# An expert layer whose third weight pass is skipped by a branch for experts of at most 64 tokens

## The chip, the cores and the metric

The kernel runs on one core of a Trainium2 chip. The metric is the device time of one execution in microseconds, from three runs. A core has five engines that run their own queues in order and signal one another through semaphores: TensorE (PE, with the weight loads shown apart as PEld), VectorE (DVE), ScalarE (ACT), GpSimd (POOL) and SyncE (SP, which here issues the loads from HBM). Matmul results land in PSUM; everything else lives in SBUF, 128 partitions wide.

## What is computed

Two layers over 256 tokens of 1024 numbers. Layer 0 is a hybrid attention and a SwiGLU; layer 1 is a gated MLP over chunks and a mixture of eight experts, of which each token takes two. The change touches the experts alone:

```python
logits = xf @ w_router                       # 256 x 8
top_val, top_idx = lax.top_k(logits, 2)
gate = softmax(top_val)
# for each expert e, over the tokens that picked it:
y_e = (silu(x_e @ w_gate[e]) * (x_e @ w_up[e])) @ w_down[e]   # 1024 -> 3584 -> 1024
# y[token] = sum of gate * y_e over the token's two experts
```

All matrices are float32. The weights of one expert are 3 x 1024 x 3584 numbers, 44.04 MB; eight experts make 352 MB, which have to come from HBM once.

The number of tokens of an expert depends on the data. Running the reference's router on the inputs that setup_inputs() draws by default gives 59, 51, 67, 65, 51, 62, 83 and 74 tokens for experts 0 to 7.

## The kernel before

Float32 products are made from two float32r parts. Each operand is split into a high part (the operand rounded by a ScalarE cast) and a low part (operand minus high part, a subtraction on VectorE or GpSimd). A product is then three passes of matmuls into the same PSUM accumulator: high x high, high x low of the weights, low of the tokens x high of the weights.

`weights` (L95 to L130) brings in one weight tile of 1 MiB, 128 partitions x 2048 columns: a load on SP's queue into the next buffer of a ring of raw tiles, a cast on ScalarE into `wh` (L123), and a subtraction into `wl` on the engine asked for (L127). `cuts` says in how many pieces the cast and the subtraction are made; in the expert layer MOE_CUTS = (1, 1), one of each. The raw tiles have a ring of 14 buffers there (4 + 7 + 1 + W_BUFS_MOE = 2), `wh` and `wl` a ring of three each (WS_BUFS). A cast has to wait until TensorE is through with the tile three before it.

An expert has 128 slots for tokens. `gather` (L828) makes the tokens of the slots by matmuls with a 0/1 matrix, splits them into `xh` and `xl`, and keeps the way back. `expert_up` (L852) works in seven slabs of 512 hidden columns: for w_gate and for w_up two weight tiles each, and for each 128 rows three matmuls with the tokens as the stationary and 512 weight columns as the moving operand, into `ps_a`; then silu on ScalarE (L865) and the product on VectorE (L866). `expert_turn` transposes the slab on TensorE (L872) and splits it into `hh` and `hl` (`split_into`, L133 and L134). `expert_down` (L878) adds the slab's part of the down product, two weight tiles and 24 matmuls, into two `ps_d` accumulators; it runs one slab behind the up products (`late_down`). So an expert takes 42 weight tiles of 12 matmuls, 504 in all. `combine` (L895) spreads the expert's rows back over the tokens; GpSimd adds them to the sum `yacc` (L911).

The matmuls of one slab and the next follow one another on TensorE; the framework's scheduler orders the instructions of each engine ahead of time by its own estimate of durations, in the program's order of priority. `run_experts` (L958) goes over the experts; the gate weights are made in slab 3 of expert 0 (GATE_SLAB), the next expert's tokens are gathered in slab 5 (GATHER_SLAB). At the end a loop with a run-time count (L999) does the experts with more than 128 tokens again; there are none here, and it is jumped over.

Of the kernel before, what the change touches and what calls it, by code (L numbers as in the profile page):

```python
# [9 lines left out]
F32 = mybir.dt.float32  # L10
# [19 lines left out]
EPS = 1e-5  # L30
NEG = -1.0e30
# [9 lines left out]
# how many of a group's four heads the scalar engine scales, for each block of queries  # L41
ASIDE = dict(a=(1, 1), w=(0, 1), s=(2, 1))
GATE_SLAB, GATHER_SLAB = 3, 5
# [7 lines left out]
def tile_hybrid_gmlp_moe(  # L51
# [23 lines left out]
    # weights: rings of 8 KB buffers (raw, and the two parts), spread over the pools that exist at the time  # L75
# [18 lines left out]
    def weights(src, a, b, lo_engine=V, loads=1, cuts=(2, 4), behind=None):  # L94
        """src as two float32r parts whose sum is src; loaded and split in as many pieces as asked for, each equal  # L95
        share of the pieces queued behind what one entry of behind has for their engine."""
# [106 lines left out]
    def mm_rows(accs, lhs_h, lhs_l, parts, first, last, done=None):  # L203
        """accs[b][half][t, 512] += x[:, k]^T w[k]; parts: (wh, wl, row chunks) of weight tiles, one block at a time."""
# [18 lines left out]
    def rows_2k(w, g, lo_engine=V):  # L223
        """rows g * 256 to g * 256 + 255 of a matrix of D columns"""
# [7 lines left out]
    def mm_cols(acc, lhs_h, lhs_l, w, js):  # L232
        """acc[col, t] = w[:, js]^T x, over the whole model dimension."""
# [13 lines left out]
    with ExitStack() as actx:  # L247
# [4 lines left out]
        # bias tables: -slope * distance, masked  # L252
# [7 lines left out]
        # compressed keys: token t against the last position of window c  # L260
# [14 lines left out]
        # sel[r, c] = 1 where r is c or c + 32: adds the two parts of a stacked product  # L275
# [41 lines left out]
        # softmax of one group of four heads over dense keys: probabilities times `scale4`, transposed  # L317
# [142 lines left out]
                # gelu(z) = z / (1 + exp(-2 sqrt(2 / pi) (z + 0.044715 z^3)))  # L460
# [83 lines left out]
        # projections and attention, in the order that keeps the tensor engine fed  # L544
# [22 lines left out]
        # output projection, residual, norm  # L567
# [15 lines left out]
    with ExitStack() as fctx:  # L583
# [29 lines left out]
        def ffn_up_blocks(s):  # L613
            """the same, one block of tokens after the other"""
# [53 lines left out]
    with ExitStack() as gctx:  # L668
# [14 lines left out]
        # with the norm's gain and shift taken into the weights, it works from what the norm is taken of  # L683
# [185 lines left out]
    def expert_turn(sg):  # L869
        pt = ps_t()  # L870
        for i in range(4):
            PE.transpose(pt[:, i * P:(i + 1) * P], sg[:, i * P:(i + 1) * P], ident)  # L872
# [170 lines left out]
```

## Time and profile before

| | |
|---|---|
| median of 3 runs | 1482.59 us (1481.17 to 1483.14) |
| span of the profiled execution, first to last instruction | 1480.9 us |
| busy share of the span: PE, DVE, ACT, POOL | 96%, 80%, 64%, 12% |
| moved from HBM | 423 MB, 287 GB/s over the span |

The span stands 1.7 us below the median; what lies around the first and the last instruction is not in it. The page cuts the span into 40 slices: attention up to about slice 5, the SwiGLU up to slice 9, the gated MLP up to slice 12, then the experts. Busy times of PE are of overlapping matmuls, so 96% is not yet a proof that TensorE is the limit; the share of the granted clock was 0.986 over the span, that is 2.4 GHz nearly throughout. POOL's last GpSimd additions of each expert (L911) stand at a fixed place of each expert's work and so mark the experts' period.

### The profile page before, as it was taken

How to read it: one execution, taken by the hardware profiler on the slowest of the kernel's cores; microseconds unless marked ns; L12 is line 12 of the kernel's file. 1: busy time of each engine (PE TensorE's matmuls, PEld its weight loads, DVE VectorE, ACT ScalarE, POOL GpSimd, SP SyncE). 2: the span in 40 equal slices, each digit the busy share in tenths (PEclk: the TensorE clock that was granted, in tenths of full speed). 3: DMA queues.
4: the chain of work that ended last, by engine and by line, in shares of the span. 5: the costliest groups of instructions: out<-in, count | busy, mean ns of one | idle time of the engine just before them, and what ended most of it. 6: DMA issues, size and time to landing. Idle time of an engine off the chain costs nothing. (4 is left out here: it accounts for less than half of the span.)

```text
span 1480.9 us, 18693 instructions
## 1 busy us (share of the span) xinstructions
PE 1426.8 (96%) x7207; PEld 1186.0 (80%) x7207; DVE 1182.6 (80%) x1265; ACT 953.0 (64%) x920; POOL 174.3 (12%) x139
## 2 busy tenths in 40 slices
PE   8899999999979999999999999999999999999995
PEld 7887899997768887888788788878878887887883
DVE  7888855558667988888888888888888878888886
ACT  5677544443436767776776777777677667767772
POOL 8521100002050101000200200020020002002000
PEclk9999999999989999999999999999999999999998
DMA  9523975556558898999999999999999999999940
GB/s 274 175 88 98 351 261 185 198 171 214 179 190 295 313 358 312 358 364 329 328 364 342 330 351 361 346 328 368 339 325 365 363 335 331 363 351 323 353 191 31
DMA packets 198847, 425.72 MB, mean 287 GB/s; under 512 B 8472, under 2 KB 44368, under 8 KB 198752
## 3 DMA queue, kind: packets, MB, share of 16 engines
q1 hardware_dynamic: 196448, 419.71, 80.2%
q0 software_dynamic: 1248, 4.24, 1.0%
q8 instruction: 58, 0.95, 0.3%
q10 hardware_dynamic: 1056, 0.53, 0.1%
q14 instruction: 37, 0.30, 0.1%
HBM read 423.40 MB, written 1.05 MB: 287 GB/s over the span
## 5 line engine op out<-in xcount | busy, mean ns | idle before, releaser
L127 DVE TENSOR_TENSOR wl<-w,wh 128x2048 fp32r<-128x2048 f32 (+1 forms) x544 | 907.4, 1696 | 189.3 <-ACT wh L123 185.8
L123 ACT CAST wh<-w 128x2048 fp32r<-128x2048 f32 (+1 forms) x462 | 766.5, 1668 | 255.9 <-PE ps_a L862 102.3
L860 PE MATMUL ps_a<-wh,xhl 128*128 128x512 f32 x896 | 356.4, 398 | 0.0
L862 PE MATMUL ps_a<-wh,xhl 128*128 128x512 f32 x896 | 354.4, 396 | 0.0
L861 PE MATMUL ps_a<-wl,xhl 128*128 128x512 f32 x896 | 354.2, 395 | 0.0
L862 PEld LDWEIGHTS ps_a<-wh,xhl 128*128 128x128 f32 x896 | 168.4, 188 | 39.5
L861 PEld LDWEIGHTS ps_a<-wl,xhl 128*128 128x128 f32 x896 | 168.5, 188 | 38.5
L860 PEld LDWEIGHTS ps_a<-wh,xhl 128*128 128x128 f32 x896 | 168.4, 188 | 38.6
L892 PE MATMUL ps_d<-wl,hh 128*128 128x512 f32 x448 | 178.8, 399 | 0.0
L893 PE MATMUL ps_d<-wh,hl 128*128 128x512 f32 x448 | 176.8, 395 | 0.0
L891 PE MATMUL ps_d<-wh,hh 128*128 128x512 f32 x448 | 167.7, 395 | 0.4 <-ACT hh L133 0.4
L911 POOL TENSOR_TENSOR yacc<-yacc,part 128x512 f32<-128x512 f32 x28 | 65.4, 2356 | 796.9 <-ACT part L910 796.9
L236 PE MATMUL ps_a<-xth,wh 128*128 128x256 f32 x448 | 128.6, 288 | 3.1 <-DVE hg L471 3.1
L238 PE MATMUL ps_a<-xth,wl 128*128 128x256 f32 x448 | 128.5, 287 | 0.8 <-DVE wl L127 0.8
L237 PE MATMUL ps_a<-xtl,wh 128*128 128x256 f32 x448 | 127.7, 285 | 0.0
L891 PEld LDWEIGHTS ps_d<-wh,hh 128*128 128x128 f32 x448 | 84.2, 188 | 20.9 <-ACT hh L133 0.9
L892 PEld LDWEIGHTS ps_d<-wl,hh 128*128 128x128 f32 x448 | 84.3, 188 | 20.1 <-DVE wl L127 1.4
L893 PEld LDWEIGHTS ps_d<-wh,hl 128*128 128x128 f32 x448 | 84.3, 188 | 18.5
L236 PEld LDWEIGHTS ps_a<-xth,wh 128*128 128x128 f32 x448 | 86.5, 193 | 4.9 <-issue 3.7
L238 PEld LDWEIGHTS ps_a<-xth,wl 128*128 128x128 f32 x448 | 86.5, 193 | 2.5 <-issue 1.2
L237 PEld LDWEIGHTS ps_a<-xtl,wh 128*128 128x128 f32 x448 | 86.5, 193 | 0.9 <-DVE xtl L134 0.2
L127 POOL TENSOR_TENSOR wl<-w,wh 128x512 fp32r<-128x512 f32 (+1 forms) x56 | 65.8, 1209 | 69.8 <-ACT wh L123 69.7
(304 smaller groups left out, 1377.9 us busy)
## 6 DMA issues: line engine op xcount, KB each, us to landing
w<-in_moe_w_gate_dram SPq DMA_DIRECT2D x112, 1024.0 KB, 6.3
w<-in_moe_w_up_dram SPq DMA_DIRECT2D x112, 1024.0 KB, 7.3
w<-in_moe_w_down_dram SPq DMA_DIRECT2D x112, 1024.0 KB, 6.8
w<-in_ffn_w_gate_dram SPq DMA_DIRECT2D x11, 1024.0 KB, 5.6
w<-in_ffn_w_up_dram SPq DMA_DIRECT2D x11, 1024.0 KB, 9.3
w<-in_ffn_w_down_dram SPq DMA_DIRECT2D x11, 1024.0 KB, 6.2
w<-in_gmlp_w_in_dram SPq DMA_DIRECT2D x8, 1024.0 KB, 5.1
w<-in_att_w_in_dram SPq DMA_DIRECT2D x7, 1024.0 KB, 6.0
```

Of the source, the lines that this page charges most:

```text
L123: S.copy(wh_f[:, sl], w_f[:, sl])
L127: ins = lo_engine.tensor_tensor(wl_f[:, sl], w_f[:, sl], wh_f[:, sl].bitcast(F32), op=OP.subtract)
L236: PE.matmul(acc, wh[:, k, js], lhs_h[:, k, :], start=k == 0, stop=False)
L237: PE.matmul(acc, wh[:, k, js], lhs_l[:, k, :], start=False, stop=False)
L238: PE.matmul(acc, wl[:, k, js], lhs_h[:, k, :], start=False, stop=k == KD - 1)
L860: PE.matmul(acc, xh[:, k, :], wh[:, i, :], start=k == 0, stop=False)
L861: PE.matmul(acc, xh[:, k, :], wl[:, i, :], start=False, stop=False)
L862: PE.matmul(acc, xl[:, k, :], wh[:, i, :], start=False, stop=k == KD - 1)
L891: PE.matmul(accs[half], hh[:, k, :], wh[:, i, hs], start=s == 0 and k == 0, stop=False)
L892: PE.matmul(accs[half], hh[:, k, :], wl[:, i, hs], start=False, stop=False)
L893: PE.matmul(accs[half], hl[:, k, :], wh[:, i, hs], start=False, stop=last and k == 3)
L911: G.tensor_tensor(yacc[:, b, hs], yacc[:, b, hs], part[:, b], op=OP.add)
```

## The change

Three things change in the expert layer.

First, a branch. For experts 1 to 7, `few` is 1 where the expert has at most 64 tokens. Slots 64 to 127 of such an expert are empty, so the low parts of its tokens are put there: `gather` and `expert_turn` add `xl` (or `hl`) of slots 0 to 63, times `few`, to slots 64 to 127 of `xh` (or `hh`). The first pass then makes high x high in rows 0 to 63 and low x high in rows 64 to 127, and `add_halves` adds the two halves (times `few`) by a ScalarE copy and a VectorE addition. The third pass stands under `tc.If(many > 0)`, where `many` is a register of TensorE alone, loaded once per expert. With the tokens above, the branch skips it for experts 1, 4 and 5. Expert 0 has no branch and no halves, and keeps three passes.

Second, slabs of 1024 hidden columns (three, and one of 512) in place of 512. Tiles stay 1 MiB and 42 per expert; the passes of a tile are now run one after the other, eight matmuls each (four per branch and half in the last slab's down part). A row of w_gate and w_up read from HBM is 4 KB instead of 2 KB, and one partition of a w_down tile is 8 KB in one piece instead of two of 4 KB. Tiles are asked for up to three ahead (`take_tile`). W_BUFS_MOE goes from 2 to 1, GATE_SLAB to 1 and GATHER_SLAB to 2.

Third, GpSimd makes the low parts of the last 384 of the 2048 columns of each tile of the expert layer (not of the first three tiles and the last one), VectorE those of the other 1664.

```diff
-W_BUFS, W_BUFS_LATE, W_BUFS_MOE, WS_BUFS = 4, 7, 2, 3
+W_BUFS, W_BUFS_LATE, W_BUFS_MOE, WS_BUFS = 4, 7, 1, 3
+MOE_ASIDE = 384
...
-            sl = slice(i * a * b // cuts[1], (i + 1) * a * b // cuts[1])
+            sl = slice(i * (a * b - aside) // cuts[1], (i + 1) * (a * b - aside) // cuts[1])
...
+        if aside:
+            sl = slice(a * b - aside, a * b)
+            G.tensor_tensor(wl_f[:, sl], w_f[:, sl], wh_f[:, sl].bitcast(F32), op=OP.subtract)
@@ in gather
+        if few is not None:
+            V.scalar_tensor_tensor(xh[:, :, HALF:], xl[:, :, 0:HALF], few, xh[:, :, HALF:], op0=OP.mult, op1=OP.add)
+            V.scalar_tensor_tensor(back[HALF:, :], pt[0:HALF, :T], few[0:HALF], back[HALF:, :], op0=OP.mult, op1=OP.add)
@@ the branch, the halves, then expert_up
+    def low_half(many):
+        return nullcontext() if many is None else tc.If(many > 0)
+
+    def add_halves(acc, tmp, few):
+        S.activation(tmp, acc[HALF:, :], AF.Copy, scale=few[HALF:])
+        V.tensor_tensor(acc[0:HALF, :], acc[0:HALF, :], tmp, op=OP.add)
...
+                for k, j, acc, hs in each:
+                    PE.matmul(acc, xh[:, k, :], wh[:, j, hs], start=k == 0, stop=False)
+                with low_half(many):
+                    for k, j, acc, hs in each:
+                        PE.matmul(acc, xl[:, k, :], wh[:, j, hs], start=False, stop=False)
+                for k, j, acc, hs in each:
+                    PE.matmul(acc, xh[:, k, :], wl[:, j, hs], start=False, stop=k == KD - 1)
...
+                for h, acc in enumerate(accs):
+                    hs = slice(h * 512, (h + 1) * 512)
+                    if few is not None:
+                        add_halves(acc, sg[0:HALF, hs], few)
+                    S.activation(sg[:, hs], acc, AF.Silu)
...
+                add_halves(acc, tmp, few)
+                V.scalar_tensor_tensor(sg[:, hs], sg[:, hs], first, acc, op0=OP.mult, op1=OP.mult)
@@ in expert_turn
+            if few is not None:
+                V.scalar_tensor_tensor(h4[:, :, HALF:], l4[:, :, 0:HALF], few, h4[:, :, HALF:], op0=OP.mult, op1=OP.add)
@@ in expert_down
+            for k, j, wh, wl, acc, hs in each:
+                PE.matmul(acc, hh[:, k, :], wh[:, j, hs], start=s == 0 and k == 0, stop=False)
+            with low_half(many):
+                for k, j, wh, wl, acc, hs in each:
+                    PE.matmul(acc, hl[:, k, :], wh[:, j, hs], start=False, stop=False)
+            for k, j, wh, wl, acc, hs in each:
+                PE.matmul(acc, hh[:, k, :], wl[:, j, hs], start=False, stop=last and k == 2 * n - 1)
...
+                    more = nc.values_load(many_i[0:1, col], engines=[mybir.EngineType.PE], min_val=0, max_val=1,
```

## Rows read from the trace of the kernel before

**Rows 1.** Each engine's busy time in two of six experts' periods.

```profile
585.73:713.22 127.49, 126.60 (x575) 102.40 (x575) 108.05 (x63) 91.67 (x66) 9.34 (x5) 1.00 0.97 346
...
1223.40:1350.63 127.23, 126.26 (x576) 102.50 (x575) 107.49 (x61) 91.69 (x66) 9.31 (x5) 1.00 0.97 347
```

**Rows 2.** TensorE in order of time, start and duration, one matmul and the 17th after.

```profile
815.84 0.40 PE L891 MATMUL ps_d<-wh,hh 128*128 128x512 f32 x1
...
819.81 0.39 PE L893 MATMUL ps_d<-wh,hl 128*128 128x512 f32 x1
```

**Rows 3.** Groups of instructions in one expert's period (713.22 to 841.24).

```profile
L127 DVE TENSOR_TENSOR wl<-w,wh 128x2048 fp32r<-128x2048 f32 x43 | 99.7, 2323 | 19.1 <-ACT wh L123 18.9
L123 ACT CAST wh<-w 128x2048 fp32r<-128x2048 f32 x42 | 80.2, 1910 | 21.9 <-PE ps_a L862 13.1 <-PE ps_d L893 8.8
L861 PE MATMUL ps_a<-wl,xhl 128*128 128x512 f32 x113 | 44.6, 395 | 0.0
L134 DVE TENSOR_TENSOR hl<-ps_t,hh 128x512 fp32r<-128x512 f32 x7 | 4.8, 683 | 0.0
L866 DVE TENSOR_TENSOR sg<-sg,ps_a 128x512 f32<-128x512 f32 x7 | 4.8, 681 | 0.9 <-PE ps_a L862 0.9
```

**Rows 4.** SP's waits from 560 to 1400 us, and DMA at work in 4 us.

```profile
SPq L108 <- DVE wl L127: 717.5, 277, 5.4
...
468.00:472.00 4.00, 4.00 (x19) 3.25 (x18) 3.96 (x2) 2.81 (x2) 0.00 (x0) 1.00 1.05 401
```

**Rows 5.** VectorE in order of time around a GpSimd addition of an expert.

```profile
584.55 2.29 DVE L127 TENSOR_TENSOR wl<-w,wh 128x2048 fp32r<-128x2048 f32 x1 [1.29 <-ACT wh L123]
586.76 0.68 DVE L134 TENSOR_TENSOR y<-ps_d,y 128x512 fp32r<-128x512 f32 x1
588.00 3.40 DVE L127 TENSOR_TENSOR wl<-w,wh 128x2048 fp32r<-128x2048 f32 x1 [0.56 <-ACT wh L123]
```

**Rows 6.** GpSimd in the same stretch, and its durations in ns: minimum, median, maximum.

```profile
585.73 3.52 POOL L911 TENSOR_TENSOR yacc<-yacc,part 128x512 f32<-128x512 f32 x2 [87.30 <-ACT part L910]
...
L911 POOL TENSOR_TENSOR yacc<-yacc,part x28: 1273/2420/3355, 585.7 to 1357.4; 128x512 f32<-128x512 f32 x28
...
L127 POOL TENSOR_TENSOR wl<-w,wh x56: 721/1288/1750, 19.3 to 438.7; 128x512 fp32r<-128x512 f32 x40, 128x256 fp32r<-128x256 f32 x16
```

**Rows 7.** GpSimd's eight 256-column subtractions, and VectorE twice on one line.

```profile
421.93 6.93 POOL L127 TENSOR_TENSOR wl<-w,wh 128x256 fp32r<-128x256 f32 x8
...
426.99 1.29 DVE L187 SCALAR_TENSOR_TENSOR x_nat<-x_nat,ln,ln_gb 128x512 f32<-128x512 f32 x1
...
432.36 0.75 DVE L187 SCALAR_TENSOR_TENSOR x_nat<-x_nat,ln,ln_gb 128x512 f32<-128x512 f32 x1 [0.30 <-POOL ln L184]
```

**Rows 8.** VectorE and ScalarE groups by shape over the whole span.

```profile
L127 DVE TENSOR_TENSOR wl<-w,wh 128x512 fp32r<-128x512 f32 x212 | 140.3, 712 | 63.6 <-ACT wh L123 60.8 <-DMA w<-in_ffn_w_up_dram 2.4
L370 DVE TENSOR_TENSOR o_t<-ps_d,o_tmp 64x256 f32<-64x256 f32 x16 | 6.6, 415 | 3.7 <-ACT o_tmp L367 3.5
L367 ACT COPY o_tmp<-ps_d 64x512 f32<-64x512 f32 x8 | 4.7, 582 | 1.7 <-PE ps_d L541 1.4 <-DVE o_t L370 0.2
```

**Rows 9.** TensorE's sequencer at the loop's end: register load and branches, durations in ns.

```profile
L997 PEldq TENSOR_LOAD <-n_over_i x1: 484/484/484, 1464.5 to 1464.5; - x1
...
L999 PEldq COMPARE_BRANCH  x3: 97/185/3303, 1465.1 to 1476.8; - x3
```

**Rows 10.** TensorE's last two matmuls, in order of time.

```profile
1464.46 0.50 PE L904 MATMUL ps_t<-y,back 128*128 128x512 f32 x1 [0.75 <-DVE yacc L907]
1464.80 0.40 PE L905 MATMUL ps_t<-y,back 128*128 128x512 f32 x1
```

More of the change, by code (lines that the diff above doesn't have):

```diff
@@ L826, in take_of, with gather @@
         return take
-    def gather(n, take):
+    def gather(n, take, few=None):
         xhl = moe.tile([P, 2, KD, P], F32R, name="xhl", tag=f"xhl{n % 2}", bufs=1)
@@ new lines, in tile_hybrid_gmlp_moe, with up_src, down_src @@
+    slabs = [(c0, min(1024, FE - c0)) for c0 in range(0, FE, 1024)]
+    def up_src(w, s, i):
+        c0, wd = slabs[s]
+        a = 2048 // wd
+        return w[i * a * P:(i + 1) * a * P, c0:c0 + wd].rearrange("(k p) c -> p k c", p=P), a, wd
+    def down_src(w, s, i):
+        r0 = slabs[s][0] + i * 256
+        return w[r0:r0 + 256, :].rearrange("(p i) c -> p i c", i=2), 2, D
+    def low_half(many):
[3 more added lines that the diff above has]
+        V.tensor_tensor(acc[0:HALF, :], acc[0:HALF, :], tmp, op=OP.add)
@@ new lines, in expert_down @@
+    def expert_down(take_tile, s, hh, hl, accs, many):
+        last = s == len(slabs) - 1
+        n = slabs[s][1] // 256
+        got = [(i, *take_tile()) for i in range(n)] if last else [None] * n
+        for tiles, hfs in [(got, (0,)), (got, (1,))] if last else [([i], (0, 1)) for i in range(n)]:
+            if not last:
+                tiles = [(tiles[0], *take_tile())]
+            each = [(2 * i + j, j, wh, wl, accs[h], halves[h]) for i, wh, wl in tiles for j in range(2) for h in hfs]
+            for k, j, wh, wl, acc, hs in each:
[5 more added lines that the diff above has]
+                PE.matmul(acc, hh[:, k, :], wl[:, j, hs], start=False, stop=last and k == 2 * n - 1)
@@ L939, in tile_hybrid_gmlp_moe @@
     n_over_i = late.tile([P, 1], I32)
+    few = late.tile([P, NE], F32)
+    first = late.tile([P, NE], F32)
+    many_i = late.tile([P, NE], I32)
     def gate_weights():
@@ L956, in gate_weights, with fetch, take_tile @@
         V.tensor_copy(n_over_i, n_over)
+        V.tensor_scalar(few, lp[:, 0:NE], HALF + 0.5, None, op0=OP.is_lt)
+        V.tensor_scalar(first, few, -1.0, 1.0, op0=OP.mult, op1=OP.add)
+        V.tensor_copy(many_i, first)
+        V.memset(first[0:HALF, :], 1.0)
     def run_experts(todo, start_acc):
-        ready = [up_weights(todo[0][0], 0, kh, G, cuts=(2, 8), behind=[after[kh]]) for kh in range(2)] if start_acc else []
+        order = []
+        behind = None
+        for n, (w_gate, w_up, w_down, _, _) in enumerate(todo):
+            for s in range(len(slabs)):
+                order += [up_src(w, s, i) for w in (w_gate, w_up) for i in range(slabs[s][1] // 256)]
+                if behind:
+                    order += behind
+                behind = [down_src(w_down, s, i) for i in range(slabs[s][1] // 256)]
+        order += behind
+        ready = []
+        at = [0]
+        def fetch(*how, **kw):
+            if at[0] < len(order):
+                src, a, b = order[at[0]]
+                at[0] += 1
+                if at[0] == len(order):
+                    kw["cuts"] = (2, 4)
+                elif not how:
+                    kw["aside"] = MOE_ASIDE
+                ready.append(weights(src, a, b, *how, **{"cuts": MOE_CUTS, **kw}))
+        def take_tile():
+            while len(ready) < WS_BUFS and at[0] < len(order):
+                fetch()
+            return ready.pop(0)
+        if start_acc:
+            for i in range(2):
+                fetch(G, cuts=(2, 8), behind=[after[i]])
         take = take_of(todo[0][3])
-        ready += [up_weights(todo[0][1], 0, kh, cuts=MOE_CUTS, behind=[marks]) for kh in range(2)] if start_acc else []
-        gathered = [gather(0, take)]
+        if start_acc:
+            fetch(behind=[marks])
+        gathered = [(*gather(0, take), None, None, None)]
         late_down = None
@@ L967, in run_experts @@
             closing = n == len(todo) - 1
-            xh, xl, back = gathered[n]
-            for s in range(n_slab):
-                sg = expert_up(w_gate, w_up, s, xh, xl, ready)
+            xh, xl, back, few_n, first_n, many = gathered[n]
+            for s in range(len(slabs)):
+                sg = expert_up(take_tile, s, xh, xl, few_n, first_n, many)
                 if late_down:
```

88 lines of the change are left out of this document (39 added, 49 removed).

## The prediction

> **What bounds the kernel now.** The order in which to read is: the busy times by stretch, then the groups of one stretch, then the order of time around one event. GpSimd's additions into yacc come once per expert, so stretches cut at them are the experts' periods: six of them take 127.2 to 128.0 us, each with TensorE busy for all but 1 us at the full granted clock (1.00, 2.4 GHz), VectorE 108 us and ScalarE 91.7 us [rows 1]. Busy matmuls overlap, so the pace is taken from starts: 17 matmuls in 819.81 - 815.84 = 3.97 us, 0.2335 us each [rows 2]. An expert's 504 make 117.7 us; 28 transposes, 32 matmuls of the gather and the way back fill the rest. TensorE sets the period. VectorE and ScalarE wait for it: a cast waits for a buffer that TensorE still reads, VectorE waits for casts (19.1 us per expert) [rows 3]. Loads are not late: SP stands waiting for a free raw buffer 717.5 of 840 us [rows 4]. So a shorter TensorE helps until the next engine is late, and that one has only 127.5 - 108 = 19.5 us of room.
>
> **The change, part by part.** *Third pass skipped.* Three of seven branching experts (1, 4, 5; at most 64 tokens) lose 504/3 = 168 matmuls, 168 x 0.2335 = 39.2 us each: TensorE would need 88 us there, 127.5 us in experts 2, 3, 6, 7 and in expert 0. All seven have the same work on the other engines, for the halves are added whether few is 1 or 0.
>
> *ScalarE.* Added: 14 copies of 64 x 512 from PSUM per expert at 0.58 us [rows 8] = 8.1 us; 91.7 + 8.1 = 99.8 us. Below 127 us, and not first.
>
> *VectorE alone.* A subtraction costs 2.29 us undisturbed for 2048 columns [rows 5] and 0.71 us on average for 512 [rows 8], 1.05 ns a column with the averages (2.32 and 0.71); 384 fewer columns save 0.40 us, leaving 1.89 us, 42 x 0.40 = 16.9 us per expert. Added: 14 additions of halves at 0.68 us (the nearest rows, an addition with PSUM of 512 columns [rows 3]) = 9.6 us; 7 additions of hl into hh, 256 columns, 0.42 us by the 64 x 256 row [rows 8] = 2.9 us; 1.1 us in the gather. 108.0 - 16.9 + 13.6 = 104.7 us.
>
> *GpSimd's 384 columns.* This is the dear part. A yacc addition of 512 columns began at 585.73 while a VectorE subtraction ran (584.55 for 2.29 us); the two additions together end at 589.25, though one alone takes 1.27 us at least [rows 5, 6]: 1 us of those 3.52 was spent waiting for the subtraction's end. The subtraction that began at 588.00, just after the second addition had started, took 3.40 us instead of 2.29: it waited 1.11 us for GpSimd [rows 5, 6]. The VectorE operation in between, which reads one operand from PSUM, took its usual 0.68 us beside GpSimd's first addition [rows 5]. So in this trace operations whose two operands are both in SBUF take turns with GpSimd, in full, and those with an operand in PSUM do not. With 256 columns of GpSimd in the way a VectorE operation took 1.29 us instead of 0.75, a wait of 0.54 us [rows 7]. Between 0.54 us for 256 and 1.11 us for 512 columns, 384 hold VectorE up for about 0.83 us (an estimate halfway). It saves 0.40 us and costs a turn of 0.83 us.
>
> Turns per expert: 42 x (1.89 + 0.83) = 114.2 us; four yacc additions at 1.11 = 4.4 us; the hh additions and one of the gather, both operands in SBUF, 3.6 us. Sum 122.2 us. VectorE's other 32 operations of 0.68 us (7 products, 7 + 4 splits, 14 halves; 21.9 us) can run in GpSimd's turns. If all do, the two engines need 122.2 us; if none does, 144.1 us. A turn of 0.83 us covers one such operation, and there are 42 turns for 32, but they come in clumps (two additions and two products at the end of each w_up, split and hh addition after it), and a clump's second and third are not covered. I take two thirds covered: 122.2 + 7.3 = 129.5 us, 2 us over today's period, in all seven experts.
>
> The Trainium skill (SBUF — State Buffer, "SBUF: two separate sides") says that of a GpSimd operation and a VectorE operation with two SBUF inputs, the one that starts first holds the shared pair of ports for its whole instruction. The rows agree that one blocks, but the wait was 1.11 us of an instruction of at least 1.27; by the page's wording a turn would be about 1.00 us, midway between the durations for 256 and 512 columns, 42 x 0.17 = 7 us more per expert, some 50 us more in all.
>
> *Experts with three passes.* TensorE's 127.5 us and the pair's 129.5 us are nearly equal and linked by three weight buffers, so each waits for the other at times: 2 us more each is my estimate from one missed cast of 1.91 us [rows 3]. Expert 0 has no halves: 42 turns and 4 us make 118 us, TensorE keeps it at 127.5.
>
> *Branches.* 42 per expert on TensorE's sequencer, never seen inside a matmul stream here. The branches at the loop took 0.10 and 0.19 us, one 3.30 us [rows 9]. The register load began at 1464.5, when the matmul of 1464.46 had just started [rows 9, 10]: the sequencer doesn't wait for matmuls to end. If it runs ahead, branches cost nothing; if each join makes it wait for the last matmul, 0.40 us (a matmul's 0.395 us [rows 3]), 16.8 us per expert. I take zero. The register load, 0.48 us seven times, is 3 us at most, at zero if ahead.
>
> *Loads.* At 122 us an expert's 44.04 MB ask for 361 GB/s; 401 was moved in a stretch of full work [rows 4]. Larger pieces don't hurt. One raw buffer of 14 fewer costs nothing: SP waits for buffers, not for data [rows 4]. SP's queue holds only these loads.
>
> *Ring of three.* Cast 1.91, VectorE 1.89, GpSimd 0.83, matmuls 1.87 us make 6.5 us over three buffers, 2.2 us per tile, below 122.2 / 42 = 2.9. The first pass needs only wh.
>
> *Sum.* Experts 1, 4, 5: +2.0 each, not -39. Experts 2, 3, 6, 7: +4.0 each. The last expert's halves in the tail: 0.58 + 0.68, about 1 us. 6 + 16 + 1 = 23 us on the profiled 1480.9, which stands 1.7 us below the median: 1504 and, on the median, 1506 us.
>
> **Rivals.**
> *A. The turns fit.* If all of VectorE's PSUM operations fall into GpSimd's turns, the pair needs 122.2 us: experts 1, 4, 5 gain 5.3 us each, the others stay. 16 us less, 1467 us. For it: 42 turns for 32 operations, and ScalarE ahead. Against: VectorE works in order.
> *B. GpSimd doesn't hold up VectorE.* Then experts 1, 4, 5 go at VectorE's 104.7 us or a few more, say 111: 3 x 16.5 = 50 us less, 1433 us. Against it stand the waits of 1.11 and 0.54 us [rows 5 to 7]. This is also the sum that leaves the turns out.
> *C. The branches stop the stream.* 0.40 us at 42 joins in experts 2, 3, 6, 7 makes TensorE 144.3 us there, 67 us in all; in 1, 4, 5 88 + 17 is still covered. With 6 us for those three 1556 us. It decides from 0.05 us per join, where TensorE's 129.6 us passes the pair's.
> *D. Each skip fetches code.* If the taken branch costs the 3.30 us of the longest branch [rows 9], experts 1, 4, 5 need 88 + 42 x 3.30 = 227 us on TensorE, 298 us more in all, about 1780 us. The Trainium skill (Runtime: NRT & Kernel Launch, "Instruction fetch mechanics") says that a taken branch whose target lies outside the instructions at hand stalls for a fetch; the row of 3.30 us is a jump over a whole expert's code, while these skip eight matmuls, so few should.
> That the branch skips nothing would need other token counts; it would change little, as the pair is the limit.
>
> **How the numbers follow.** Forecast 0.53 (of it 0.07 within 0.2%, the smallest difference that a measurement of this kernel can tell), A 0.20, B 0.10, C 0.12, D 0.05. Faster by over 0.2%: A and B, 0.30. Same 0.07. Slower 0.46 + 0.12 + 0.05 = 0.63. The forecast's own range is 1485 (a quarter of the 21.9 us uncovered, no further waits) to 1540 (six tenths uncovered). The range goes from 1455 (A with 3 us more hidden in four experts) to 1568 (C with the register loads and some misses), leaving out B and D.
>
> **What would show it.** VectorE's 1664-column subtractions well above 1.89 us where they wait, GpSimd's above 1.0; experts 1, 4 and 5 no more than 5 us shorter than now, with TensorE idle a quarter of them and waiting for wl; the other experts 127 to 135 us. Wrong would be: undisturbed 1.89 us beside a working GpSimd and short periods of about 111 us (B), or gaps at the branch in TensorE's order of time (C, D).

## The result, and the profile after

The changed kernel takes 1543.6 us (median of four runs, 1541.6 to 1546.1) beside 1482.9 for the kernel before on the same chip: 1.0412 times as long (95% interval 1.0397 to 1.0428), 61 us more. Forecast was 1506 us, 23 more. The direction was right and the time lies in the range given, 1455 to 1568, but outside the forecast's own, 1485 to 1540, and 38 us of the loss are not in the sum.

Where it went, by expert: the time from the first up matmul of an expert to that of the next (for expert 7 to the end of the span), in us.

| expert | 0 | 1 | 2 | 3 | 4 | 5 | 6 | 7 to end |
|---|---|---|---|---|---|---|---|---|
| tokens | 59 | 51 | 67 | 65 | 51 | 62 | 83 | 74 |
| before | 119.0 | 127.5 | 127.3 | 127.5 | 127.3 | 127.3 | 127.2 | 149.8 |
| after | 120.4 | 125.2 | 135.5 | 136.6 | 140.1 | 134.4 | 138.4 | 165.4 |

Expert 0, without branch and halves but with the new slabs and GpSimd's share, stayed. Experts 2, 3 and 6 lost 8 to 11 us where 4 were forecast. Of the three that skip a third of their matmuls, 1 gained 2.3 and 4 and 5 lost 12.8 and 7.1, where 2 each were forecast. Expert 7 with the end of the kernel lost 15.6, the largest single part, where 5 were forecast.

The page of the changed kernel, busy times and the granted clock in 40 slices:

```profile
PE 1390.3 (90%) x6703; PEld 1085.7 (70%) x6703; DVE 1277.5 (83%) x1427; ACT 1004.5 (65%) x1017; POOL 903.6 (59%) x472
...
PEclk9999999999989999999999999999999999999997
```

Each engine's busy time in experts 2 and 4 of the changed kernel, which answer to [rows 1], and in two stretches of 8 us inside expert 4 (columns as there: stretch, its length, PE, PEld, DVE, ACT, POOL, clock, DMA share, GB/s):

```profile
692.16:827.68 135.52, 129.30 (x567) 99.78 (x566) 124.20 (x86) 99.03 (x79) 101.80 (x47) 1.00 0.89 328
964.27:1104.38 140.11, 111.42 (x416) 71.93 (x415) 122.47 (x86) 98.96 (x79) 99.60 (x47) 0.95 0.87 319
...
1000.00:1008.00 8.00, 5.01 (x18) 3.71 (x18) 3.96 (x4) 3.51 (x6) 7.13 (x5) 0.75 0.65 209
1008.00:1016.00 8.00, 6.29 (x19) 3.59 (x17) 7.16 (x7) 5.86 (x6) 2.83 (x2) 0.83 0.53 179
```

VectorE is busy 124.2 and 122.5 us here. That this is near the forecast's 122.2 for the pair is chance: VectorE's busy time holds the 22 us of operations with PSUM that the forecast's sum leaves out, and not the turns of GpSimd that VectorE did not wait for. What that sum means is the time in which GpSimd runs or VectorE runs an operation without PSUM. Counted from the start and end of each instruction in the trace it is 122.3 us in expert 2 and 123.8 in expert 4, so the sum was met. VectorE's PSUM operations add 9.3 and 10.6 us outside that time, where the forecast has 7.3 (two thirds covered), and for another 3.9 and 5.7 us neither engine works: 135.5 and 140.1 in all. A period read as the largest engine sum plus a third of the unhidden work misses what the engines wait for one another. From 1000 to 1008, just where expert 3's rows are spread back, VectorE is idle half the time and GpSimd alone is busy.

Groups of expert 4 in the changed kernel, which answer to [rows 3]:

```profile
L131 DVE TENSOR_TENSOR wl<-w,wh 128x1664 fp32r<-128x1664 f32 x43 | 98.9, 2331 | 9.8 <-ACT wh L127 9.4 <-issue 0.4
L136 POOL TENSOR_TENSOR wl<-w,wh 128x384 fp32r<-128x384 f32 x43 | 94.0, 2202 | 37.8 <-ACT wh L127 30.2 <-PE ps_a L893 5.9 <-PE ps_d L937 1.6
L875 ACT ACTIVATE tmp<-ps_a,few 64x512 f32<-64x512 f32 x7 | 4.8, 686 | 6.1 <-PE ps_a L893 6.0
L876 DVE TENSOR_TENSOR ps_a<-ps_a,tmp 64x512 f32<-64x512 f32 x7 | 4.8, 682 | 0.0
L924 DVE SCALAR_TENSOR_TENSOR hh<-hl,few,hh 128x256 fp32r<-128x256 f32 x7 | 4.8, 690 | 0.1
```

and VectorE's subtractions over the experts, minimum, median and maximum in ns:

```profile
L131 DVE TENSOR_TENSOR wl<-w,wh x281: 1871/2679/2953, 570.3 to 1477.6; 128x1664 fp32r<-128x1664 f32 x141
```

VectorE's subtraction of 1664 columns takes 2.33 us against 1.89 undisturbed. Where it waits, it mostly waits 0.8 us (2.68 at the median for 1.87 at the least), the turn that was forecast, but it waits at about every second tile, so 0.44 us a tile. The other side of the turn is the dearer one: GpSimd's 384 columns, 0.99 us at the least (below), take 2.20 us on average. The halves cost what was forecast, but for the copies (0.68 for 0.58 us) and the hh additions (0.69 for 0.42, turns among them).

What the engines of the changed kernel waited for from 600 to 1480 us (engine, what, for whom; us in total, times, longest):

```profile
PEld ps_a L893 <- DVE wl L131: 70.2, 82, 2.7
ACT hh L140 <- PE ps_d L942: 66.7, 19, 5.7
ACT sg L875 <- PE ps_a L893: 61.8, 20, 4.2
DVE wl L131 <- ACT wh L127: 56.0, 62, 4.2
ACT tmp L875 <- PE ps_a L893: 43.8, 23, 2.4
...
ACT part L959 <- POOL yacc L960: 23.7, 7, 4.8
...
PEld ps_t L920 <- ACT part L959: 20.0, 7, 5.0
...
PEld ps_t L920 <- PEq L938: 10.2, 14, 0.8
```

and in the kernel before, in the same stretch:

```profile
PEld ps_t L872 <- ACT part L910: 8.2, 6, 1.4
...
PEld ps_d L892 <- DVE wl L127: 1.4, 9, 0.2
```

Two circles can be read from these lines. In the first, ScalarE waits at the head of its queue for TensorE to finish a slab (66.7, 61.8 and 43.8 us for hh, sg and tmp), the casts behind it come late, VectorE waits for casts, and TensorE for VectorE. In the second, once per expert, ScalarE's copies into the one buffer of `part` wait for GpSimd's yacc additions, and TensorE's transposes wait for ScalarE to empty `ps_t`. The second is not new: the kernel before has the same wait, 1.4 us at the most where it is now up to 5.0.

The second circle in order of time, expert 4 of the changed kernel, which answers to [rows 5, 6]:

```profile
996.88 2.72 POOL L136 TENSOR_TENSOR wl<-w,wh 128x384 fp32r<-128x384 f32 x1 [3.75 <-PE ps_a L893]
...
999.56 4.15 POOL L960 TENSOR_TENSOR yacc<-yacc,part 128x512 f32<-128x512 f32 x2
...
1003.67 0.99 POOL L136 TENSOR_TENSOR wl<-w,wh 128x384 fp32r<-128x384 f32 x1
1003.74 1.26 ACT L959 ACTIVATE part<-ps_t,gate 128x512 f32<-128x512 f32 x2 [3.58 <-POOL yacc L960]
...
1004.48 1.98 PE L920 MATMUL ps_t<-ident,sg 128*128 128x128 f32 x8 [2.84 <-ACT part L959]
...
1006.27 0.69 DVE L141 TENSOR_TENSOR hl<-ps_t,hh 128x512 fp32r<-128x512 f32 x1 [3.68 <-ACT hh L140]
```

GpSimd's additions stand behind a share of 2.72 us and take turns with VectorE themselves; ScalarE stops for 3.58 us, TensorE for 2.84, VectorE for 3.68. In the kernel before GpSimd had nothing else to do there.

### The profile page after: what moved, and what is told of

It reads as the page before. It is cut to its first block, busy times and chain, and to the rows that moved or that the text cites. A ratio compares the mean times of both kernels' runs of the same rounds, so it can differ in the third digit from the quotient of the medians.

```text
span 1542.6 us, 19479 instructions
## 1 busy us (share of the span) xinstructions
PE 1390.3 (90%) x6703; PEld 1085.7 (70%) x6703; DVE 1277.5 (83%) x1427; ACT 1004.5 (65%) x1017; POOL 903.6 (59%) x472
## 5 line engine op out<-in xcount | busy, mean ns | idle before, releaser
L131 DVE TENSOR_TENSOR wl<-w,wh 128x1664 fp32r<-128x1664 f32 (+1 forms) x541 | 899.1, 1700 | 150.4 <-ACT wh L127 144.2
L136 POOL TENSOR_TENSOR wl<-w,wh 128x384 fp32r<-128x384 f32 x333 | 743.0, 2248 | 272.5 <-ACT wh L127 245.7
L127 ACT CAST wh<-w 128x2048 fp32r<-128x2048 f32 (+1 forms) x461 | 751.6, 1671 | 134.9 <-PE ps_d L653 25.2
L893 PE MATMUL ps_a<-wl,xhl 128*128 128x512 f32 x896 | 272.2, 419 | 42.8 <-DVE wl L131 38.0
L888 PE MATMUL ps_a<-wh,xhl 128*128 128x512 f32 x896 | 258.1, 405 | 8.8 <-ACT wh L127 8.6
L888 PEld LDWEIGHTS ps_a<-wh,xhl 128*128 128x128 f32 x896 | 168.5, 192 | 57.3 <-ACT wh L127 23.5
L891 PE MATMUL ps_a<-wh,xhl 128*128 128x512 f32 x560 | 153.6, 395 | 0.0
L191 POOL TENSOR_TENSOR ln<-ln,neg_half 128x1 f32<-128x1 f32 x10 | 9.6, 961 | 243.0 <-DVE ln L190 243.0
L942 PE MATMUL ps_d<-wl,hh 128*128 128x512 f32 x448 | 132.9, 416 | 16.4 <-DVE wl L131 11.4
L937 PE MATMUL ps_d<-wh,hh 128*128 128x512 f32 x448 | 127.7, 405 | 14.3 <-ACT wh L127 9.5
L891 PEld LDWEIGHTS ps_a<-wh,xhl 128*128 128x128 f32 x560 | 105.4, 188 | 24.5
L140 ACT CAST hh<-ps_t 128x512 fp32r<-128x512 f32 (+1 forms) x58 | 31.9, 581 | 79.9 <-PE ps_d L942 74.0
```

Source lines behind the costliest of these rows:

```text
L127: S.copy(wh_f[:, sl], w_f[:, sl])
L136: G.tensor_tensor(wl_f[:, sl], w_f[:, sl], wh_f[:, sl].bitcast(F32), op=OP.subtract)
L140: marks[S] = S.copy(hi, src)
L888: PE.matmul(acc, xh[:, k, :], wh[:, j, hs], start=k == 0, stop=False)
L891: PE.matmul(acc, xl[:, k, :], wh[:, j, hs], start=False, stop=False)
L893: PE.matmul(acc, xh[:, k, :], wl[:, j, hs], start=False, stop=k == KD - 1)
```

## The experiments

Theory T is the forecast's: the turns of VectorE and GpSimd are the loss. Its rivals changed as results came in. All runs were timed beside the kernel before (1481.6 to 1482.2 us); the ratio's 95% interval stands in brackets.

**Without GpSimd's share.** The line of the first is all its edit; in the second GpSimd writes zeros, so the low parts of these columns are left out.

```diff
-MOE_ASIDE = 384
+MOE_ASIDE = 0
@@ zeros_aside, in weights
-            G.tensor_tensor(wl_f[:, sl], w_f[:, sl], wh_f[:, sl].bitcast(F32), op=OP.subtract)
+            G.memset(wl_f[:, sl].bitcast(F32), 0.0)
```

> The changed kernel with all 2048 columns of the low parts on VectorE (GpSimd's share 0). Theory T (VectorE and GpSimd take turns and their joint work sets the experts' period): VectorE gains 42 x 0.40 = 17 us of work per expert and loses about as much waiting (18.5 us in expert 4), so the time stays within 15 us of the changed kernel's 1543.6: 1530 to 1555 us. Rival R1 (GpSimd's turns are the whole loss, VectorE alone has room): 1470 to 1500 us. Rival R2 (branches or the chain of the halves are the loss): 1535 to 1555 us, TensorE's waits for wl as long as now.

1512.2 us, 1.0203 [1.0186, 1.0220]: between the range of T and that of R1. The share costs 31 us; half of the loss is there without it.

> The changed kernel, but GpSimd writes zeros into the last 384 columns of wl instead of the subtraction; so the low parts of these columns' weights are left out of the products. GpSimd still writes 384 columns per tile and VectorE still does 1664, but GpSimd reads nothing. Theory T: VectorE's 1664-column subtractions fall from 2.33 to about 1.89 us, experts 1, 4, 5 take 115 to 122 us, the others 128 to 131: 1470 to 1500 us. Rival R2 (branches or the halves' chain): nothing gained, over 1525 us. If a write alone blocks VectorE as well, 1520 us or more with VectorE's subtractions still above 2.1 us.

1485.4 us, 1.0026 [1.0016, 1.0036], in T's range. VectorE's subtractions are back at 1.90 us although GpSimd still writes 384 columns per tile (expert 4):

```profile
L131 DVE TENSOR_TENSOR wl<-w,wh 128x1664 fp32r<-128x1664 f32 x42 | 78.5, 1904 | 13.2 <-ACT wh L127 7.6 <-POOL wl L136 4.5 <-issue 1.1
...
L136 POOL MEMSET wl<- 128x384 f32 x42 | 17.6, 420 | 97.7 <-PE ps_a L893 59.5 <-PE ps_d L942 34.6 <-DVE wl L131 3.7
```

With 384 columns off VectorE and no turns at the tiles, the changed kernel is 58 us faster and still no faster than the kernel before.

**Without branch and halves.** No expert gets `few`, `first` or `many`; slabs and pass order stay.

```diff
-                    got = gather(n + 1, take_of(todo[n + 1][3]), few[:, col])
+                    got = gather(n + 1, take_of(todo[n + 1][3]))
...
-                    gathered.append((*got, few[:, col], first[:, col], more))
+                    gathered.append((*got, None, None, None))
```

> Slabs of 1024 and GpSimd's 384 columns, but no branch and no halves: all experts make three passes, as expert 0 does in the changed kernel. Theory T: turns of 42 x 2.72 + 5 = 119 us plus some 4 us of uncovered PSUM operations stay under TensorE's 127.5 us: 1480 to 1495 us. Rival R1 (the turns alone): 1520 us or more. Rival R2 (branch or halves): 1480 to 1490 us.

1524.4 us, 1.0289 [1.0272, 1.0306]. T missed; the time lies in R1's range, but the next run shows that the share is 18 us of it and not the whole.

> Slabs of 1024 alone: no branch, no halves, nothing on GpSimd. All theories: TensorE sets 127.5 us per expert, 1478 to 1488 us. Over 1495 us the slabs or the order of the passes would themselves cost something.

1506.4 us, 1.0165 [1.0149, 1.0182]. Every theory missed: slabs of 1024 and the new pass order, which the forecast's sum has no term for, lose 25 us by themselves. ScalarE in order of time in this kernel (bracket: idle time before, and for whom):

```profile
951.53 0.59 ACT L140 CAST hh<-ps_t 128x512 fp32r<-128x512 f32 x1 [5.08 <-PE ps_t L920]
952.02 7.32 ACT L127 CAST wh<-w 128x2048 fp32r<-128x2048 f32 x4
962.90 1.09 ACT L901 ACTIVATE sg<-ps_a 128x512 f32<-128x512 f32 x2 [3.56 <-PE ps_a L893]
```

and in the kernel before:

```profile
949.56 0.59 ACT L133 CAST hh<-ps_t 128x512 fp32r<-128x512 f32 x1 [1.33 <-PE ps_t L872]
950.05 1.91 ACT L123 CAST wh<-w 128x2048 fp32r<-128x2048 f32 x1
952.36 1.91 ACT L123 CAST wh<-w 128x2048 fp32r<-128x2048 f32 x1 [0.40 <-PE ps_a L862]
955.16 0.60 ACT L865 ACTIVATE sg<-ps_a 128x512 f32<-128x512 f32 x1 [0.89 <-PE ps_a L862]
```

Before, casts and evictions alternate and each waits about a microsecond. After, the scheduler has put evictions ahead of casts that could have run: ScalarE stands 5.08 us and then makes four casts on end. By the trace, TensorE's last matmuls on the buffers that the first two of these casts refill (its low x high passes) ended at 947.3 and 950.1, 4.7 and 1.9 us before ScalarE got to the first cast. Experts 1 and 2, whose instructions stand in another order, ran at 126.5 and 126.2 us; experts 3 to 6, ordered as here, at 131.2 to 132.3.

**Which part of the slabs.** From three_passes_vector_alone: slabs of 512 (and with them the old places of the gate weights and of the gather), the old pass order, both, or tiles asked for one at a time.

```diff
-    slabs = [(c0, min(1024, FE - c0)) for c0 in range(0, FE, 1024)]
+    slabs = [(c0, 512) for c0 in range(0, FE, 512)]
-GATE_SLAB, GATHER_SLAB = 1, 2
+GATE_SLAB, GATHER_SLAB = 3, 5
@@ old pass order, in expert_up; expert_down alike
                 for k, j, acc, hs in each:
                     PE.matmul(acc, xh[:, k, :], wh[:, j, hs], start=k == 0, stop=False)
+                    PE.matmul(acc, xh[:, k, :], wl[:, j, hs], start=False, stop=False)
+                    PE.matmul(acc, xl[:, k, :], wh[:, j, hs], start=False, stop=k == KD - 1)
@@ tiles one at a time, in take_tile
-            while len(ready) < WS_BUFS and at[0] < len(order):
+            while len(ready) < 1 and at[0] < len(order):
```

> The changed kernel with slabs of 512 columns in place of 1024, three passes for every expert without branch and halves, VectorE alone for the low parts; of the change only the order of the passes, the fetching up to three tiles ahead and the two row orders are left. W (the 25 us of three_passes_vector_alone come from the width of the slabs: its evictions come in clumps of two and stand in ScalarE's queue ahead of casts): 1478 to 1488 us, experts 3 to 6 back at 126 to 128 us. O (they come from the order of the passes or from the fetching ahead): still 1498 to 1510 us, experts 3 to 6 at 131 to 133 us.

1497.3 us, 1.0098 [1.0081, 1.0115]: between W and O.

> three_passes_vector_alone with the three matmuls of each 128 rows and half one after the other, as in the kernel before, in place of three passes of eight. W (width): 1500 to 1512 us. O (order of the passes): 1478 to 1488 us.

1494.1 us, 1.0081 [1.0065, 1.0098]: between as well.

> Slabs of 512 columns and the three matmuls of each 128 rows one after the other, both as in the kernel before; three passes for all experts, VectorE alone. Of the change only the fetching of tiles up to three ahead, 13 raw buffers in place of 14 and the row order of w_down are left. F (the fetching ahead puts the casts in another place of ScalarE's queue, and that is the common part of the loss): 1490 to 1497 us, experts 3 to 6 at 129 to 131. Rival (width and pass order each carry a part of the 25 us and nothing else does): 1479 to 1486 us.

1483.9 us, 1.0013 [1.0003, 1.0022]; experts 2 to 6 at 127.3 to 127.7. The rival held: width and pass order together make 22.5 us, and each alone only gives back 9 or 12.

> three_passes_vector_alone (slabs of 1024, passes one after the other, 1506 us) with each tile asked for only when its matmuls are written down, in place of up to three ahead. F: 1480 to 1490 us. Rival (slabs of 1024 and passes of eight lose by themselves): 1498 to 1512 us.

1506.4 us, 1.0161 [1.0144, 1.0178]: nothing. F fell, here and with branch and halves:

> vector_alone (branch and halves, no share for GpSimd, 1512 us) with each tile asked for only when its matmuls are written down. F: about 20 us faster, 1485 to 1497 us. Rival: 1505 to 1520 us. If the halves' evictions wait for TensorE at the head of ScalarE's queue all the more: slower than 1520.

1512.4 us, 1.0198 [1.0180, 1.0216].

**Branch and halves.** The second run keeps vector_alone and passes None for `few_n` and `first_n` to expert_up and expert_turn.

```diff
-        return nullcontext() if many is None else tc.If(many > 0)
+        return nullcontext() if many is None else tc.If(many < 2)
@@ branch_without_halves, with MOE_ASIDE = 0
-                sg = expert_up(take_tile, s, xh, xl, few_n, first_n, many)
+                sg = expert_up(take_tile, s, xh, xl, None, None, many)
...
-                hh, hl = expert_turn(sg, s, few_n)
+                hh, hl = expert_turn(sg, s, None)
```

> The changed kernel with the branch's condition many < 2 in place of many > 0: the same instructions, but the second pass is never skipped. Experts 1, 4 and 5 then also add the low parts of their tokens a second time, so their output is off by that. P (VectorE, GpSimd and the casts set the period whether TensorE skips or not): 1535 to 1560 us, experts 1, 4 and 5 within 6 us of the changed kernel's 125.2, 140.1 and 134.4. Rival (the skip gains as much as its 39 us of TensorE allow, and something else costs more): 1570 us or more. If a skipped pass itself costs time (a jump in TensorE's queue): under 1530 us.

1553.0 us, 1.0479 [1.0461, 1.0496]. P held: skipping 504 matmuls, 3 x 39.2 = 118 us of TensorE, gains 9.5 us. Experts 1, 4 and 5 took 130.9, 136.6 and 136.7, so in the two profiled executions the skip gives these three 4.5 us together, and expert 4 is slower with it; 3.6 us of the difference lie ahead of the first expert.

> The changed kernel with VectorE alone for the low parts (as vector_alone, 1512 us) and the branch kept, but what the halves add left out: the ScalarE copies and VectorE additions of the two halves of the up products and the addition of hl into hh. The rows 64 to 127 of experts with at most 64 tokens are then wrong. H (the halves' work on ScalarE and VectorE, and their places in the queues, eat what the skip gives): experts 1, 4 and 5 at 108 to 116 us, 1450 to 1475 us. Rival (the branch or a falling clock of TensorE eats it): experts 1, 4 and 5 at 122 us or more, 1490 us or more.

1483.0 us, 1.0013 [1.0003, 1.0023]; experts 1, 4, 5 at 110.5, 121.5 and 121.5, the others that branch at 133.3. Between the two. Against vector_alone the halves cost 29 us, 6 to 9 in each of experts 1, 4, 5 and 7 (its end included) and up to 3 in experts 2, 3 and 6. Against three_passes_vector_alone the branch gains 23 us in all: 11 to 16 in each expert that skips, while 2, 3 and 6 lose 7, 2 and 1.

> The changed kernel with slabs of 512 columns and VectorE alone for the low parts: the branch and the halves are kept. If the loss of 25 us by the slabs of 1024 and the 6 us that branch and halves cost beside VectorE alone stand apart: 1512 - 25 = 1487 us (1480 to 1494), experts 1, 4, 5 at 120 to 125 us and the others at 128 to 132. If the halves' evictions in ScalarE's queue are the loss whatever the width: 1505 to 1520 us. If nothing but VectorE's 121 us sets experts 1, 4 and 5 and TensorE the others: 1460 to 1470 us.

1542.9 us, 1.0411 [1.0382, 1.0440]. All three ranges missed, those from sums of separate terms among them: the narrow slab that is better with three passes is 31 us worse with the halves. Terms of this kernel don't add.

**GpSimd's queue.** In yacc_on_vector, from the changed kernel:

```diff
-                    S.activation(part[:, b], pt, AF.Copy, scale=gate_of(b))
-                    G.tensor_tensor(yacc[:, b, hs], yacc[:, b, hs], part[:, b], op=OP.add)
+                    V.scalar_tensor_tensor(yacc[:, b, hs], pt, gate_of(b), yacc[:, b, hs], op0=OP.mult, op1=OP.add)
```

> The changed kernel with one step moved: VectorE adds the spread rows to yacc straight from PSUM, in place of a ScalarE copy into part and a GpSimd addition. Q (the yacc additions stand in GpSimd's queue behind its shares of the weights, ScalarE waits for the one buffer of part and TensorE for ScalarE: 20.0 us of TensorE's waits in seven places, and about as much again until VectorE is fed): 15 to 35 us faster than the changed kernel, 1508 to 1528 us. Rival (the stall at the end of an expert only takes the place of a wait that VectorE and GpSimd would make anyway): 1536 to 1550 us.

1511.0 us, 1.0188 [1.0166, 1.0211]: 33 us faster, in Q's range. Four operations per expert moved off GpSimd and ScalarE undo as much as the removal of all 42 shares. TensorE's wait for `part` is gone, while the turns at the tiles are nearly the same (expert 4):

```profile
L131 DVE TENSOR_TENSOR wl<-w,wh 128x1664 fp32r<-128x1664 f32 x43 | 97.0, 2284 | 7.6 <-ACT wh L127 7.6
L136 POOL TENSOR_TENSOR wl<-w,wh 128x384 fp32r<-128x384 f32 x43 | 96.5, 2262 | 36.0 <-ACT wh L127 30.2 <-PE ps_a L893 5.7
```

The edit takes away two things at once, the chain through `part` and the additions' own turns: the time in which GpSimd runs or VectorE runs an operation without PSUM falls from 123.8 to 118.9 us in expert 4, about as much as the period (140.1 to 134.4). Which of the two the 33 us are, this run does not tell; a second buffer for `part` alone was not tried. TensorE also waits 8.4 us for `part` in vector_alone, where no share stands ahead, so only 12 of the 20.0 us come with the share.

The share alone, in the kernel before (the same two hunks of `weights`, aside=384 for its tiles):

> The kernel before with one thing of the change alone: GpSimd makes the low parts of the last 384 columns of each weight tile of the expert layer but the first four and the last two. By the forecast's terms VectorE and GpSimd need 42 x 2.72 + 4.4 + 1.8 = 120.4 us per expert and a third of 18 operations of 0.68 us, 4.1 us, 124.5 us: below TensorE's 127.5, so 1480 to 1488 us. If a turn costs more than the forecast's 0.83 us, as the 18 us between three_passes and three_passes_vector_alone suggest: 1494 to 1506 us, with GpSimd's 384 columns at about 2 us each and VectorE's 1664 columns at 2.3.

1536.3 us, 1.0360 [1.0338, 1.0382]: 54 us from the share alone, where the forecast's terms give none; both ranges missed. The pair's part of those terms was met: by the same count expert 4 has 118.6 us of turns and 5.9 of PSUM operations outside them, 124.5 as expected and less than TensorE's 127.5. Yet its period is 136.1. Its waits in expert 4:

```profile
ACT hh L136 <- PE ps_d L896: 15.3, 4, 3.8
...
PEld ps_t L875 <- ACT part L914: 4.2, 1, 4.2
ACT part L914 <- POOL yacc L915: 4.0, 1, 4.0
```

The same with the yacc edit above:

> share_of_384_in_kernel_before (1536 us) with the yacc additions on VectorE straight from PSUM, in place of ScalarE's part and GpSimd's addition. Q (the yacc additions behind GpSimd's shares are the larger part of the loss there too, 3.8 us of TensorE's waits at one place per expert and what follows from it): 1495 to 1515 us. Rival (the turns at each tile are the loss): 1525 to 1540 us.

1498.6 us, 1.0108 [1.0091, 1.0125]. In Q's range again: 38 of the 54 us go with the additions; 17 stay for the turns and the rest. Since the pair was below TensorE's time here, the chain is the likelier reading, but TensorE's waits for `part` from 560 to 1480 us are 28.5 us for 9.6 in the kernel before: 19 of the 38 are seen directly, and the rest, as what follows from them, is argued.

**Buffers.**

```diff
-W_BUFS, W_BUFS_LATE, W_BUFS_MOE, WS_BUFS = 4, 7, 1, 3
+W_BUFS, W_BUFS_LATE, W_BUFS_MOE, WS_BUFS = 2, 7, 1, 4
```

> The changed kernel with four buffers for wh and wl in place of three (WS_BUFS = 4, W_BUFS = 2, the same room; tiles are asked for four ahead). L (casts that stand late in ScalarE's queue and turns on GpSimd hurt because only three tiles are under way, so a wait of 3 to 6 us reaches TensorE): 1490 to 1525 us. Rival (VectorE and GpSimd are the limit by their own work, so no buffer helps): 1532 to 1550 us.

1556.4 us, 1.0517 [1.0477, 1.0558]. L fell. With two raw buffers fewer the first expert starts 8 us later (454.8 for 446.6); from there the profiled execution, which at 1548.1 us is 8 under the median, takes 1091.6 us for 1096.1. No gain of 20 to 50.

**A better order.** Two tries, with no share for GpSimd and slabs of 1024 or 512:

```diff
                 for k, j, acc, hs in each:
                     PE.matmul(acc, xh[:, k, :], wh[:, j, hs], start=k == 0, stop=False)
+                    if j < a - 1:
+                        PE.matmul(acc, xh[:, k, :], wl[:, j, hs], start=False, stop=False)
                 with low_half(many):
...
                 for k, j, acc, hs in each:
+                    if j == a - 1:
-                    PE.matmul(acc, xh[:, k, :], wl[:, j, hs], start=False, stop=k == KD - 1)
+                        PE.matmul(acc, xh[:, k, :], wl[:, j, hs], start=False, stop=k == KD - 1)
```

> vector_alone (branch and halves, no share for GpSimd, slabs of 1024, 1512 us) with the products with wl next to those with wh of the same rows, as in the kernel before; only those of a tile's last rows stand behind the branch. G (passes of eight lose 12 us by where the scheduler then puts the evictions, with the branch as without): 1495 to 1503 us, experts 2, 3 and 6 at 130 to 133. Rival (with the halves the evictions are late anyway): 1507 to 1518 us.

1592.7 us, 1.0747 [1.0729, 1.0765].

> The same order in slabs of 512 columns (branch_in_slabs_512 took 1543 us). G, together with the width, as in the three-pass kernels: 1478 to 1495 us, experts 1, 4 and 5 at 120 to 124 and the others at 128 to 130. Rival (in slabs of 512 the halves' copies wait for TensorE with nothing else of the slab left to do, whatever the order of the passes): 1530 us or more.

1643.5 us, 1.1073 [1.1026, 1.1120]. In the first both ranges missed; in the second G missed, and the rival's "1530 us or more" holds. TensorE's waits in the first from 570 to 1400 us:

```profile
PEld ps_a L890 <- DVE wl L131: 62.2, 51, 2.1
...
PEld ps_a L896 <- issue: 48.1, 81, 0.8
...
PEld ps_d L948 <- issue: 24.6, 42, 0.8
```

and its weight loads in order of time in expert 4 there:

```profile
1002.17 0.30 PEld L890 LDWEIGHTS ps_a<-wl,xhl 128*128 128x128 f32 x2 [2.03 <-DVE wl L131]
1002.51 0.42 PEld L888 LDWEIGHTS ps_a<-wh,xhl 128*128 128x128 f32 x2
1003.49 0.30 PEld L896 LDWEIGHTS ps_a<-wl,xhl 128*128 128x128 f32 x2 [0.56 <-issue]
```

wl is wanted right behind the first products with wh, and VectorE's lateness reaches TensorE (62.2 us at L890 in 51 waits). And a join now costs (48.1 + 24.6) / 123 = 0.59 us in the experts that skip. But most of the loss against vector_alone lies elsewhere: 49 of 79 us of the profiled executions in experts 2, 3, 6 and 7, which skip nothing, and 30 in experts 1, 4 and 5, less than their 73 us of joins, which so take the place of other waits. In the order of the change four matmuls on wh stand ahead of the branch and the wait for wl behind it, where here two stand between that wait and the branch, and the same "issue" waits sum to 6.8 and 5.2 us from 600 to 1480:

```profile
PEld ps_a L893 <- issue: 6.8, 13, 0.6
...
PEld ps_d L942 <- issue: 5.2, 8, 0.8
```

No version beat the kernel before.

## Why the prediction was right and wrong

**Right.** TensorE set the old period and no longer sets the new one: never_skips is 9.5 us from the changed kernel. The pair needs what the forecast's sum says, 119 to 124 us in experts 2 to 6 for 122.2, and its turn of 0.83 us is what VectorE mostly waits where it waits. The turn of about 1.00 us that the prediction sets beside it, with some 50 us more in all, comes nearer the measured time only by chance. Expert 0 is unchanged. Rival B: VectorE does wait (2.33 for 1.89 us), and without the waits, in zeros_aside, the kernel takes 1485 and not B's 1433. Rivals C and D: no compare-and-branch took the 3.30 us of [rows 9]; a skip jumps over four matmuls (504 / 3 / 42), not eight. Joins are not free, but far from C's 67 us: behind a skipped pass the weight loads wait 12 us in all for "issue", and 10.2 us in 14 places where the transposes stand right behind a branch of the down products (PEq L938, above); never_skips, whose passes all run, has none of either beyond 0.2 us. The branches of the up products, and the register load:

```profile
L889 PEldq COMPARE_BRANCH  x308: 65/174/336, 564.9 to 1496.3; - x154
...
L1072 PEldq TENSOR_LOAD <-many_i x7: 302/309/482, 564.3 to 1376.3; - x7
```

**Wrong, in three steps.** First, the sum has no term for slabs and pass order: it looked at bytes, buffers and counts, all unchanged. They alone cost 25 us with three passes. An order planned ahead is part of the kernel; a new shape is a new order on every engine, and ScalarE's queue then stands for evictions with casts behind them. That this order is the cause is read from ScalarE's order of time; no run put the casts back.

Second, "I take two thirds covered: 122.2 + 7.3 = 129.5 us", with "2 us more each" for engines that wait for one another, in the experts with three passes alone. The 122.2 us were met. Of VectorE's 22 us of PSUM operations 9.3 to 11.0 stayed uncovered in experts 2 to 6, not 7.3, and for 3.9 to 5.7 us neither engine worked, where 0 to 2 were allowed. That is 134 to 140 us a period for 129.5 to 131.5. Without any share the skipping experts 4 and 5 still took 129.0 and 127.7 us, and without halves 121.5, though no engine is busy more than 107 us there (expert 4 of branch_without_halves):

```profile
945.89:1067.40 121.51, 102.06 (x415) 69.87 (x414) 106.65 (x64) 88.91 (x65) 7.33 (x4) 1.00 0.95 352
```

So near a balance of TensorE, VectorE and ScalarE with three weight buffers the engines' waits for one another, not the largest sum, set the period. Four buffers did not help, so the ring's depth is not shown to be the cause.

Third, "four yacc additions at 1.11 = 4.4 us": they were priced as turns of VectorE alone. They are also a link in a chain (ScalarE's `part`, GpSimd, ScalarE, `ps_t`, TensorE) and now stand behind the shares in GpSimd's queue. In the changed kernel they are worth 33 us, 4.7 for each of the seven experts that have them (with ScalarE's four copies of 0.685 us, which went with them). That is near the 4.4 of the sum, so the size was right there, if only by luck where the chain is the cause. In the kernel before it fails: the same terms stay below TensorE's 127.5 us and give nothing, and the additions behind a share cost 38 us. The forecast gave what is queued behind the weights' subtractions on VectorE, and not on GpSimd.

The parts, one after another: slabs and pass order 1481.6 to 1506.4 (+25), the branch without halves to 1483.0 (-23), the halves to 1512.2 (+29), the share to 1543.6 (+31). The steps hold in this order only; branch_in_slabs_512 shows that.

**Open.** By what rule the scheduler places evictions ahead of casts in experts 3 to 6 was not seen; an order written by hand was not tried. Why slabs of 512 lose with the halves (TensorE waited 37.1 us for casts at L888 there, 20.1 in vector_alone) is not settled, nor all of the loss of the last two orders in experts that don't skip. Expert 7 with the end lost 7.5 us by slabs and pass order alone; what the rest of its 15.6 us are was not followed.

## What to carry to other kernels

Work given to an idle engine moves whatever that engine already does: look at who waits at the end of the chain of the small operations in its queue, and not at their duration alone. Four additions per expert cost 38 us in the kernel before with the share, where the sums of the engines gave nothing. When instruction order is planned by a scheduler, a change of tile shape needs a run with that alone before anything is built on it. A pass skipped on one engine is worth only the distance to the next circle of waits, here 9.5 of 118 us. And a busy time that equals a forecast sum is no proof of it: ask first which operations each of the two counts.

## What the runs showed of the hardware

A waiting GpSimd need not get the next turn. In expert 4 of the changed kernel, GpSimd, VectorE and those who wait:

```profile
1090.57 11.09 POOL L136 TENSOR_TENSOR wl<-w,wh 128x384 fp32r<-128x384 f32 x4 [3.10 <-ACT wh L127]
1090.59 5.48 DVE L131 TENSOR_TENSOR wl<-w,wh 128x1664 fp32r<-128x1664 f32 x3
...
1096.96 1.90 ACT L127 CAST wh<-w 128x2048 fp32r<-128x2048 f32 x1 [2.87 <-POOL wl L136]
1096.98 0.79 PE L942 MATMUL ps_d<-wl,hh 128*128 128x512 f32 x1 [3.49 <-POOL wl L136]
```

and GpSimd's shares over the experts, minimum, median and maximum in ns:

```profile
L136 POOL TENSOR_TENSOR wl<-w,wh x282: 987/2660/6361, 567.9 to 1477.6; 128x384 fp32r<-128x384 f32 x141
```

The first of the four shares took 6.36 us, 5.4 more than its own 0.99: the length of VectorE's three subtractions in a row. ScalarE and TensorE waited for it 2.87 and 3.49 us. It is rare: the only one of its kind among the experts' shares here, while yacc_on_vector has four of 5.7 to 6.4 us. The Trainium skill (SBUF — State Buffer, "SBUF: two separate sides") says that whichever of the two starts first has the shared pair of ports for its whole instruction and the other fully blocks. The blocking agrees with this trace; that the blocked one may wait through three instructions, the page does not say, and by one subtraction of 1.89 us the share would have ended after 2.9. VectorE's usual wait of 0.8 us is a little less than the share's whole 0.99. A GpSimd operation that only writes did not hold VectorE up: beside 42 memsets of 0.42 us per expert in zeros_aside its subtractions took 1.90 us.

TensorE's granted clock fell where the chain stopped it: 0.75 and 0.83 on average in the stretches of 1000 and 1008 us above, half and a third of them at 1.2 GHz, the rest at 2.4. TensorE had waited 2.84 us for ScalarE there and was busy 5.0 and 6.3 of 8 us. The kernel before had 1.00 in [rows 1].

A branch whose pass is not skipped cost nothing that the waits show (never_skips). Behind skipped passes TensorE's weight loads waited 22 us in all in the changed kernel, where four matmuls stand ahead of each branch, and 0.59 us at each of 123 joins, 73 us in all, in low_weights_first_1024, where two stand between the wait for wl and the branch.
